# Hybrid decoder layer with expert retrieval: spare weight tiles first, fewer gathers beside the out-projection, one-hot rows on POOL, ids by a minimum

## Chip, cores and metric

The kernel runs on one core of one Trainium2 chip. The metric is the device time of one execution in microseconds (us), as a median over runs.

## What is computed

One decoder layer on 512 tokens of width 2048, in float32. Two token mixers of 16 heads each (latent attention with a rotary key, and forgetting attention) run side by side; their gated outputs are joined and projected, and an expert mixer with product keys follows.

```python
merged = jnp.concatenate([y_a, y_b], axis=-1) * gates          # (1, 512, 4096)
x = x + jnp.einsum('bse,ed->bsd', merged, w_out)               # 4096 -> 2048
h = rms_norm(x, ffn_norm_g)
q = (h @ w_q).reshape(T, 8, 2, 128)
scores = jnp.einsum('thcd,hcnd->thcn', q, sub_keys)            # 128 keys a half
s1, i1 = lax.top_k(scores[:, :, 0], 16)
s2, i2 = lax.top_k(scores[:, :, 1], 16)
top_scores, top_pos = lax.top_k(all 256 sums s1 + s2, 16)
experts = take_along_axis(i1 * 128 + i2, top_pos)              # of 16384 experts
gates = softmax(top_scores)
a = einsum('td,thkd->thk', h, u[experts])
x = x + einsum('thk,thkd->td', gates * gelu(a), v[experts])
```

## The kernel before, in words

Every matrix product is done with both operands split into a high and a low part, three matmuls each (mm3, L134). A weight tile of 128x1024 is loaded by SyncE (load, L97) into a slot "raw"; each half of 512 columns is cast by ACT to whi (L108), and DVE writes the rest to wlo (L113). There are three slots always, and spare (L607) opens two more for phase 2, with a split buffer of their own; loads go round over the five.

Phase 1 runs the attention heads; each head's gated output goes to DRAM (mrg, L319). Phase 2 (L561) is the out-projection. It handles the first block of 128 tokens apart: out0_units (L685) makes 128 units of three matmuls of 512 columns over all heads, the first 96 (early) of heads that are done first, the rest (late) after the last fourth of mrg was brought in. The other 384 tokens need 128 wide units ("main", out_units, L649), nine matmuls each; FEW of these stand among the late units. After the first block's norm come its queries, top-16 searches and expert choice (select, L802), with wide units between, and then the remaining main units. During them each half of a weight tile adds RATE to a credit (half_lo, L111), and each whole credit issues a gather: POOL fetches one expert row per token of the first block (1 MB), and DVE takes its dot product with the normalized input (L951) into aa. The credit begins at -LAG x RATE, and the last REST units issue no gather. All gathers that are left (352 in all) are spread over phase 4.

Phase 3 (L851) normalizes the other 384 tokens: DVE scales into hb (L869), PE transposes into tp, ACT and DVE split into dh and dl (L94, L95); then come queries and top-16 searches. select turns positions among 80 candidates into ids: for either key half a 128x6x16x16 tile is compared with the numbers 0 to 15 (L836), multiplied by the ids (L838) and summed over the last axis (L840).

Phase 4 begins with gate_matrix (L1006), whose order of instructions is that of the code. The ids and gates are transposed to "lists" (L1013, L1015). Then 84 groups of four tokens each: DVE compares the first id with 0 to 127 for three tokens (L1026), and for the fourth multiplies by the gate as well (L1028); it compares the second id for all four (L1030); ACT scales the first three (L1032); PE multiplies (L1045); ACT copies the result out (L1046); and once per four groups POOL copies eight rows to G (L1048) while the rest goes to DRAM. Between the groups LEFT "ahead" units (12 matmuls of 336 columns of the next product) are put in. Of 56 such units, FIRST = 32 run in phase 3, LEFT in the gate matrix, and the others after it. What follows is the product with all 16384 experts for 336 tokens, gated by that matrix.

Of the kernel before, what the change touches and what calls it, by code (L numbers as in the profile page):

```python
# [13 lines left out]
AF = mybir.ActivationFunctionType  # L14
OP = mybir.AluOpType
AX = mybir.AxisListType.X
# [3 lines left out]
P = 128  # L20
# [11 lines left out]
NKEY = 128  # L32
NEXP = NKEY * NKEY
TOPK = 16
# [17 lines left out]
ND = 3  # L52
# [10 lines left out]
NRAW2 = 2  # L63
NSP2 = 3
NC = 80
GATHERS = 2 * (128 + NX)
RATE = 0.46
REST = 10
LAG = 10
AHEAD = 14  # L70
# [3 lines left out]
FEW = 4  # L74
WAIT = 6
EACH = 8
FIRST = 32
LEFT = 4 * AHEAD - FIRST - 3
# [3 lines left out]
class Kern:  # L82
# [40 lines left out]
    def half(self, w, i):  # L123
        return self.half_lo(*self.half_hi(w, i))
# [436 lines left out]
    def phase2(self, res, sm):  # L561
        nc, a = self.nc, self.a
# [11 lines left out]
        with self.pool(name="mgr", bufs=1) as self.mgr, self.pool(name="msp", bufs=3) as self.msp, \  # L574
                self.pool(name="tka", bufs=1) as tk, self.spare(NRAW2, NSP2), \
# [3 lines left out]
            main = [f for q in range(4) for f in self.out_units(q, range(1, NT))]  # L579
# [105 lines left out]
    def out0_units(self, tk, main):  # L685
# [34 lines left out]
        out = early[:40] + [self.bare(own)] + early[40:64] + half(0) + early[64:] + [self.bare(bring, 3)]  # L720
        for i in range(0, len(late), 8):
            out += late[i:i + 8] + main[i // 8:i // 8 + 1] + (half(1) if i == 8 else [])
        return out
# [78 lines left out]
    def select(self, tk, vals, ids, n, gt, ie, eqs):  # L802
# [4 lines left out]
        nc.vector.tensor_copy(idf, ids)  # L807
        cand = tk.tile([P, n, NC // 8, 8], F32, name="cand")
# [25 lines left out]
        nc.vector.tensor_tensor(out=pf[:, 1], in0=slot, in1=w, op=OP.add)  # L834
        for c, eq in enumerate(eqs):
            nc.vector.tensor_tensor(out=eq, in0=pf[:, c, :, :, None].to_broadcast(bc),  # L836
                                    in1=iota[:, None, None, :].to_broadcast(bc), op=OP.is_equal)
            nc.vector.tensor_tensor(out=eq, in0=eq, in1=idf[:, c, :, None, :].to_broadcast(bc), op=OP.mult)  # L838
        for c, eq in enumerate(eqs):
            nc.vector.tensor_reduce(out=ie[:, c], in_=eq.rearrange("p (t h) a b -> p t h a b", t=nt), op=OP.add, axis=AX)  # L840
# [165 lines left out]
    def gate_matrix(self, pool, acc, ahead):  # L1006
        nc = self.nc
        lists = pool.tile([P, 3, TD], F32, name="lists")
        for b in range(ND):
            for j in range(3):  # L1010
                src = self.gt[:, b] if j == 2 else self.ie[:, j, b]
                tp = acc.tile([P, P], F32, name="acc")
                nc.tensor.transpose(tp, src.rearrange("p h k -> p (h k)"), self.ident)  # L1013
                o = NX if b == 0 else 0
                nc.scalar.copy(lists[:, j, b * P + o - NX:b * P + P - NX], tp[:, o:])  # L1015
        iota = self.cst[:, C_I2:C_I2 + P]
# [3 lines left out]
        b3 = [P, 3, NKEY]  # L1020

        def pick(g):
            t0 = 4 * g
            o1 = pool.tile(bc, F32, name="o1", bufs=3)
            o2 = pool.tile(bc, F32, name="o2", bufs=3)
            nc.vector.tensor_tensor(out=o1[:, :3], in0=lists[:, 0, t0:t0 + 3, None].to_broadcast(b3),  # L1026
                                    in1=iota[:, None, :].to_broadcast(b3), op=OP.is_equal)
            nc.vector.tensor_scalar(out=o1[:, 3], in0=iota, scalar1=lists[:, 0, t0 + 3:t0 + 4],  # L1028
                                    scalar2=lists[:, 2, t0 + 3:t0 + 4], op0=OP.is_equal, op1=OP.mult)
            nc.vector.tensor_tensor(out=o2, in0=lists[:, 1, t0:t0 + 4, None].to_broadcast(bc), in1=it, op=OP.is_equal)  # L1030
            for i in range(3):
                nc.scalar.activation(o1[:, i], o1[:, i], AF.Copy, scale=lists[:, 2, t0 + i:t0 + i + 1])  # L1032
            return o1, o2
# [252 lines left out]
```

## Time and profile before

| | |
|---|---|
| median of 3 runs | 4154.52 us (4152.19 to 4154.86) |
| the profiled execution | 4157.29 us, span 4155.5 us |
| mean granted clock | 0.989 |
| busy: PE, DVE, ACT, POOL | 4035.3, 3138.3, 1899.2, 642.0 us |
| attention, to about 1470 us | then the first out-projection to about 1612 us |
| main units with gathers | about 1700 to 1931 us |
| phase 3 | about 1931 to 2184 us |
| gate matrix | about 2184 to 2310 us |
| phase 4's products | to the end |

PE's busy time counts matmuls whose ends are modelled. An engine's idle time matters where PE waits for it; a gap of PE is read from the row that follows it, with the instruction that ended the wait. The rows are from one profiled execution, so sums are made against its own time.

### The profile page before, as it was taken

What the parts mean: (1) busy time and instruction counts of PE and PEld (TensorE: products, weight loads), DVE (VectorE), ACT (ScalarE), POOL (GpSimd) and SP (SyncE); (2) the same over time, 40 slices, a digit from 0 to 9 for tenths busy, and PEclk for the clock granted to TensorE, in tenths of its full rate; (3) what the DMA queues carried; (4) which work ended last, traced back from release to release, by engine and by line L of the source; (5) the groups of instructions that cost most, each with busy time, mean ns of one, the idle gap of its engine ahead of it and who ended that gap; (6) DMA issues with size and microseconds to landing.
All of it is one profiled execution on the core that took longest, in us unless ns stands there. A gap on an engine that the chain in (4) does not pass through costs nothing. (4 is left out here: it accounts for less than half of the span.)

```text
span 4155.5 us, 61144 instructions
## 1 busy us (share of the span) xinstructions
PE 4035.3 (97%) x22575; PEld 3633.3 (87%) x22575; DVE 3138.3 (76%) x5377; ACT 1899.2 (46%) x3677; POOL 642.0 (15%) x531
## 2 busy tenths in 40 slices
PE   8999999999999978998989999999999999999999
PEld 6878888888888756776989999999999999999998
DVE  8555655655555567888999888888888888888886
ACT  4555555555555555433339533333333333333332
POOL 1111101111111100022001112112221222122120
PEclk9999999999999989999999999999999999999999
DMA  3222222222222277698337898889889989899896
GB/s 134 88 77 82 79 82 82 86 74 85 81 86 79 84 265 261 245 357 319 116 118 201 313 341 334 338 340 348 336 332 347 339 334 347 343 327 356 323 340 211
DMA packets 246924, 937.94 MB, mean 226 GB/s; under 512 B 23760, under 2 KB 70864, under 8 KB 197840
## 3 DMA queue, kind: packets, MB, share of 16 engines
q1 hardware_dynamic: 190944, 550.11, 38.0%
q0 software_dynamic: 52160, 375.94, 23.9%
q10 hardware_dynamic: 3520, 7.98, 0.6%
q8 instruction: 177, 2.90, 0.3%
q14 instruction: 123, 1.01, 0.1%
HBM read 895.75 MB, written 38.14 MB: 225 GB/s over the span
## 5 line engine op out<-in xcount | busy, mean ns | idle before, releaser
L108 ACT CAST whi<-raw 128x512 fp32r<-128x512 f32 x1820 | 1111.1, 622 | 1745.7 <-PE acc L138 615.9
L113 DVE TENSOR_TENSOR wlo<-raw,whi 128x512 fp32r<-128x512 f32 x1820 | 1219.1, 687 | 523.4 <-ACT whi L108 510.9
L137 PE MATMUL acc<-Wh,whi 128*128 128x336 f32 x2048 | 642.2, 317 | 7.3 <-DVE x L1121 4.6
L138 PE MATMUL acc<-Wl,whi 128*128 128x336 f32 x2048 | 644.4, 316 | 0.0
L137 PE MATMUL a<-dh,whi 128*128 128x336 f32 x1984 | 629.2, 317 | 0.8 <-ACT whi L108 0.8
L138 PE MATMUL a<-dl,whi 128*128 128x336 f32 x1984 | 626.5, 316 | 0.0
L139 PE MATMUL a<-dh,wlo 128*128 128x336 f32 x1984 | 621.2, 316 | 0.9 <-DVE wlo L113 0.9
L139 PE MATMUL acc<-Wh,wlo 128*128 128x336 f32 x2048 | 607.7, 318 | 11.5 <-DVE wlo L113 11.0
L137 PE MATMUL mm<-hh,whi 128*128 128x512 f32 x1424 | 570.8, 401 | 8.3 <-ACT hh L540 8.3
L138 PE MATMUL mm<-hl,whi 128*128 128x512 f32 x1424 | 569.0, 400 | 6.5 <-DVE hl L541 6.4
L139 PE MATMUL mm<-hh,wlo 128*128 128x512 f32 x1424 | 569.1, 400 | 0.0
L137 PEld LDWEIGHTS acc<-Wh,whi 128*128 128x128 f32 x2048 | 384.8, 188 | 10.5 <-issue 6.6
L139 PEld LDWEIGHTS acc<-Wh,wlo 128*128 128x128 f32 x2048 | 375.7, 188 | 17.7 <-DVE wlo L113 17.5
L138 PEld LDWEIGHTS acc<-Wl,whi 128*128 128x128 f32 x2048 | 386.3, 189 | 0.0
L137 PEld LDWEIGHTS a<-dh,whi 128*128 128x128 f32 x1984 | 372.7, 188 | 2.2 <-ACT whi L108 1.4
L138 PEld LDWEIGHTS a<-dl,whi 128*128 128x128 f32 x1984 | 372.9, 188 | 0.0
L139 PEld LDWEIGHTS a<-dh,wlo 128*128 128x128 f32 x1984 | 371.3, 188 | 1.4 <-DVE wlo L113 1.4
L138 PEld LDWEIGHTS mm<-hl,whi 128*128 128x128 f32 x1424 | 268.6, 189 | 73.5 <-DVE hl L541 11.7
L137 PEld LDWEIGHTS mm<-hh,whi 128*128 128x128 f32 x1424 | 269.4, 189 | 67.8 <-ACT hh L540 8.3
L139 PEld LDWEIGHTS mm<-hh,wlo 128*128 128x128 f32 x1424 | 268.8, 189 | 60.9 <-issue 0.2
L951 DVE CUSTOM_DVE_ANT_0 rows<-rows,h 128x2048 f32<-128x2048 f32 x128 | 292.1, 2283 | 13.8 <-DMA rows<-u,eidx 13.8
L963 DVE SCALAR_TENSOR_TENSOR x<-rows,aa,x 128x2048 f32<-128x2048 f32 x128 | 300.1, 2345 | 0.0
(389 smaller groups left out, 6135.5 us busy)
## 6 DMA issues: line engine op xcount, KB each, us to landing
raw<-ut SPq DMA_DIRECT2D x256, 512.0 KB
raw<-vt SPq DMA_DIRECT2D x256, 512.0 KB
raw<-w_in SPq DMA_DIRECT2D x178, 512.0 KB
raw<-w_out SPq DMA_DIRECT2D x128, 512.0 KB
raw<-w_pq SPq DMA_DIRECT2D x64, 512.0 KB
gd<-rows SPq DMA_DIRECT2D x21, 1024.0 KB
G<-gd SPq DMA_DIRECT2D x15, 1344.0 KB
raw<-w_up SPq DMA_DIRECT2D x24, 512.0 KB
```

Source lines behind the costliest of these rows:

```text
L108: self.nc.scalar.copy(hi, src)
L113: ins = self.nc.vector.tensor_tensor(out=lo, in0=src, in1=hi.bitcast(F32), op=OP.subtract)
L137: nc.tensor.matmul(out, wh, xh, start=start, stop=False)
L138: nc.tensor.matmul(out, wh, xl, start=False, stop=False)
L139: nc.tensor.matmul(out, wl, xh, start=False, stop=stop)
L951: nc.vector.tensor_tensor_reduce(out=row, in0=row, in1=self.h0, scale=1.0, scalar=0.0, op0=OP.mult, op1=OP.add, accum_out=self.aa[:, k:k + 1])
L963: nc.vector.scalar_tensor_tensor(out=self.x1[0], in0=row, scalar=self.aa[:, k:k + 1], in1=self.x1[0], op0=OP.mult, op1=OP.add)
```

## The change

- The spare pool is opened before the other pools of phase 2, so that its tiles lie elsewhere in memory and the load order of the first tiles changes.
- Eight wide units (FEW) instead of four stand among the units of the first out-projection, one after every twelfth from the 36th on; the two halves of merged heads that they need are split at units 8 and 28.
- RATE is 0.40 instead of 0.46, and REST 14 instead of 10.
- select forms 256 times the position less (256 times the number plus the id), takes the absolute value on ACT and the minimum over the last axis, instead of a comparison, a multiplication and a sum.
- The lists are made in the order of kind and then of block, with an ahead unit after the second and the third kind. LEFT is 16 instead of 21.
- In the gate matrix POOL writes rows 2 and 3 of the first comparison together with the gate; DVE writes rows 0 and 1, which ACT scales.

```diff
@@ -64,18 +64,18 @@
 NSP2 = 3
 NC = 80
 GATHERS = 2 * (128 + NX)
-RATE = 0.46
-REST = 10
+RATE = 0.40
+REST = 14
 LAG = 10
 AHEAD = 14
 KEEP = 11
 LOOK = 1
 FIRST_W = {0: (0, 0), 2: (1, 0), 4: (0, 1), 6: (1, 1)}
-FEW = 4
+FEW = 8
 WAIT = 6
 EACH = 8
 FIRST = 32
-LEFT = 4 * AHEAD - FIRST - 3
+LEFT = 4 * AHEAD - FIRST - 8
 HALVES = 4 * NKEY + 4 * (NKEY - AHEAD) - 20
 
 
@@ -571,8 +571,8 @@
         self.gt = sm.tile([P, ND, PH, TOPK], F32, name="gt")
         self.ie = sm.tile([P, 2, ND, PH, TOPK], F32, name="ie")
         self.ss = sm.tile([P, NT, 4], F32, name="ss")
-        with self.pool(name="mgr", bufs=1) as self.mgr, self.pool(name="msp", bufs=3) as self.msp, \
-                self.pool(name="tka", bufs=1) as tk, self.spare(NRAW2, NSP2), \
+        with self.spare(NRAW2, NSP2), self.pool(name="mgr", bufs=1) as self.mgr, \
+                self.pool(name="msp", bufs=3) as self.msp, self.pool(name="tka", bufs=1) as tk, \
                 self.pool(name="pa", bufs=2, space=PSUM) as self.pa, \
                 self.pool(name="acc", bufs=6, space=PSUM) as self.accp:
             self.mhalf = {}
@@ -717,10 +717,18 @@
         for q in range(3):
             bring(q)
         half = lambda i: [self.bare(self.merged_half, 0, i)]
-        out = early[:40] + [self.bare(own)] + early[40:64] + half(0) + early[64:] + [self.bare(bring, 3)]
-        for i in range(0, len(late), 8):
-            out += late[i:i + 8] + main[i // 8:i // 8 + 1] + (half(1) if i == 8 else [])
-        return out
+        out, todo = [], main[:FEW]
+        for i, f in enumerate(early + late):
+            if i == len(early):
+                out.append(self.bare(bring, 3))
+            if i in (8, 28):
+                out += half(i // 20)
+            if i == 40:
+                out.append(self.bare(own))
+            out.append(f)
+            if i >= 36 and i % 12 == 0 and todo:
+                out.append(todo.pop(0))
+        return out + todo
 
     def inv_rms(self, pool, blocks, name):
         nc = self.nc
@@ -805,6 +813,9 @@
         nt = gt.shape[1]
         idf = tk.tile([P, 2, n, TOPK], F32, name="idf")
         nc.vector.tensor_copy(idf, ids)
+        nc.vector.scalar_tensor_tensor(out=idf.rearrange("p s n k -> p (s n) k"), scalar=2.0 * NKEY,
+                                       in0=iota[:, None, :].to_broadcast([P, 2 * n, TOPK]),
+                                       in1=idf.rearrange("p s n k -> p (s n) k"), op0=OP.mult, op1=OP.add)
         cand = tk.tile([P, n, NC // 8, 8], F32, name="cand")
         bc = [P, n, TOPK, TOPK]
         v1, v2 = vals[:, 0], vals[:, 1]
@@ -832,12 +843,13 @@
         nc.vector.tensor_tensor(out=w, in0=w, in1=lw, op=OP.subtract)
         nc.vector.tensor_scalar(out=slot, in0=slot, scalar1=1.0, scalar2=8.0, op0=OP.is_equal, op1=OP.mult)
         nc.vector.tensor_tensor(out=pf[:, 1], in0=slot, in1=w, op=OP.add)
+        nc.vector.tensor_scalar(out=pf, in0=pf, scalar1=2.0 * NKEY, scalar2=None, op0=OP.mult)
         for c, eq in enumerate(eqs):
             nc.vector.tensor_tensor(out=eq, in0=pf[:, c, :, :, None].to_broadcast(bc),
-                                    in1=iota[:, None, None, :].to_broadcast(bc), op=OP.is_equal)
-            nc.vector.tensor_tensor(out=eq, in0=eq, in1=idf[:, c, :, None, :].to_broadcast(bc), op=OP.mult)
+                                    in1=idf[:, c, :, None, :].to_broadcast(bc), op=OP.subtract)
+            nc.scalar.activation(eq, eq, AF.Abs)
         for c, eq in enumerate(eqs):
-            nc.vector.tensor_reduce(out=ie[:, c], in_=eq.rearrange("p (t h) a b -> p t h a b", t=nt), op=OP.add, axis=AX)
+            nc.vector.tensor_reduce(out=ie[:, c], in_=eq.rearrange("p (t h) a b -> p t h a b", t=nt), op=OP.min, axis=AX)
         b3 = [P, n, TOPK]
         g = tk.tile([P, n, TOPK], F32, name="g")
         nc.vector.tensor_tensor(out=g, in0=tv, in1=tv[:, :, 0:1].to_broadcast(b3), op=OP.subtract)
@@ -1006,29 +1018,32 @@
     def gate_matrix(self, pool, acc, ahead):
         nc = self.nc
         lists = pool.tile([P, 3, TD], F32, name="lists")
-        for b in range(ND):
-            for j in range(3):
+        for j in range(3):
+            for b in range(ND):
                 src = self.gt[:, b] if j == 2 else self.ie[:, j, b]
                 tp = acc.tile([P, P], F32, name="acc")
                 nc.tensor.transpose(tp, src.rearrange("p h k -> p (h k)"), self.ident)
                 o = NX if b == 0 else 0
                 nc.scalar.copy(lists[:, j, b * P + o - NX:b * P + P - NX], tp[:, o:])
+            if j:
+                next(ahead)
         iota = self.cst[:, C_I2:C_I2 + P]
         bc = [P, 4, NKEY]
         it = iota[:, None, :].to_broadcast(bc)
 
-        b3 = [P, 3, NKEY]
+        b2 = [P, 2, NKEY]
 
         def pick(g):
             t0 = 4 * g
             o1 = pool.tile(bc, F32, name="o1", bufs=3)
             o2 = pool.tile(bc, F32, name="o2", bufs=3)
-            nc.vector.tensor_tensor(out=o1[:, :3], in0=lists[:, 0, t0:t0 + 3, None].to_broadcast(b3),
-                                    in1=iota[:, None, :].to_broadcast(b3), op=OP.is_equal)
-            nc.vector.tensor_scalar(out=o1[:, 3], in0=iota, scalar1=lists[:, 0, t0 + 3:t0 + 4],
-                                    scalar2=lists[:, 2, t0 + 3:t0 + 4], op0=OP.is_equal, op1=OP.mult)
+            nc.vector.tensor_tensor(out=o1[:, :2], in0=lists[:, 0, t0:t0 + 2, None].to_broadcast(b2),
+                                    in1=iota[:, None, :].to_broadcast(b2), op=OP.is_equal)
+            for i in (2, 3):
+                nc.gpsimd.tensor_scalar(out=o1[:, i], in0=iota, scalar1=lists[:, 0, t0 + i:t0 + i + 1],
+                                        scalar2=lists[:, 2, t0 + i:t0 + i + 1], op0=OP.is_equal, op1=OP.mult)
             nc.vector.tensor_tensor(out=o2, in0=lists[:, 1, t0:t0 + 4, None].to_broadcast(bc), in1=it, op=OP.is_equal)
-            for i in range(3):
+            for i in range(2):
                 nc.scalar.activation(o1[:, i], o1[:, i], AF.Copy, scale=lists[:, 2, t0 + i:t0 + i + 1])
             return o1, o2
```

SyncE's queue at the start of the first out-projection, before (DMASW are loads and stores that POOL issued; the fifth row is the tile that the first unit needs):

```order
L101 DMA raw<-w_out 128x1024 [waits DMAHW7_50,DMASW0_50,DVE_50]
L101 DMA raw<-w_out 128x1024 [waits DMAHW0_50,DMASW1_50,DVE_50]
L101 DMA raw<-w_out 128x1024 [waits DMAHW1_50,DMAHW5_50,DMASW2_50,DVE_50]
L101 DMA raw<-w_out 128x1024 [waits DMAHW3_50,DVE_50]
L101 DMA raw<-w_out 128x1024 [waits DMASW5_50,DMASW4_50,DMAHW2_50,DVE_50,Pool_50]
L101 DMA raw<-w_out 128x1024 [waits Pool_50]
```

and with the change:

```order
L101 DMA raw<-w_out 128x1024 [waits Pool_50]
L101 DMA raw<-w_out 128x1024 [waits PE_50]
L101 DMA raw<-w_out 128x1024 [waits DMAHW5_50,DMAHW7_50,DMASW0_50,DVE_50]
L101 DMA raw<-w_out 128x1024 [waits DMAHW0_50,DMASW1_50,DVE_50]
L101 DMA raw<-w_out 128x1024 [waits DMAHW1_50,DMASW2_50,DVE_50]
L101 DMA raw<-w_out 128x1024 [waits DMAHW3_50,DVE_50]
```

The two tiles of the spare slots moved from fifth and sixth to first and second, and wait for POOL and for PE instead of for POOL's stores and loads.

DVE around the norm of phase 3, before (ISA rows,aa is one dot of a gathered row; n1r the norm; hb, dl and dh as in phase 3):

```order
L951 ISA rows,aa<-rows,h_14565 128x2048
L951 ISA aa 128x1
L729 TENSOR_REDUCE n1r<-ss 128x3
L148 SCALAR_TENSOR_TENSOR rsq<-n1r,rsq 128x3
L150 TENSOR_TENSOR n1y<-n1y,rsq 128x3
L869 SCALAR_TENSOR_TENSOR hb<-x_13376,n1y,hb 128x512 x3
L951 ISA rows,aa<-rows,h_14565 128x2048
L951 ISA aa 128x1
L951 ISA rows,aa<-rows,h_14565 128x2048
L951 ISA aa 128x1
L95 TENSOR_TENSOR dl<-tp,dh 128x384 x3
L113 TENSOR_TENSOR wlo<-raw,whi 128x512
```

and with the change:

```order
L963 ISA rows,aa<-rows,h_14626 128x2048
L963 ISA aa 128x1
L678 TENSOR_TENSOR x_13376<-x_13376,acc 128x512 x3
L737 TENSOR_REDUCE n1r<-ss 128x3
L148 SCALAR_TENSOR_TENSOR rsq<-n1r,rsq 128x3
L150 TENSOR_TENSOR n1y<-n1y,rsq 128x3
L881 SCALAR_TENSOR_TENSOR hb<-x_13376,n1y,hb 128x512 x3
L95 TENSOR_TENSOR dl<-tp,dh 128x384 x3
L113 TENSOR_TENSOR wlo<-raw,whi 128x512
L95 TENSOR_TENSOR dl<-tp,dh 128x384
L881 SCALAR_TENSOR_TENSOR hb<-x_13376,n1y,hb 128x512 x3
L113 TENSOR_TENSOR wlo<-raw,whi 128x512 x3
```

All dots now stand ahead of the norm; in the rows before, nine stood behind it, the last ones between later pieces of hb and dl.

DVE in the gate matrix, before (o is either one-hot tile, by its number):

```order
L1026 TENSOR_TENSOR o_19962<-lists,cst 128x384
L1028 TENSOR_SCALAR o_19962<-cst,lists 128x128
L1030 TENSOR_TENSOR o_19963<-lists,cst 128x512
L1026 TENSOR_TENSOR o_19970<-lists,cst 128x384
L1028 TENSOR_SCALAR o_19970<-cst,lists 128x128
L1030 TENSOR_TENSOR o_19971<-lists,cst 128x512
```

and with the change, DVE first:

```order
L1040 TENSOR_TENSOR o_19989<-lists,cst 128x256
L1045 TENSOR_TENSOR o_19990<-lists,cst 128x512
L1040 TENSOR_TENSOR o_19997<-lists,cst 128x256
L1045 TENSOR_TENSOR o_19998<-lists,cst 128x512
L1040 TENSOR_TENSOR o_20006<-lists,cst 128x256
L1045 TENSOR_TENSOR o_20007<-lists,cst 128x512
```

and POOL, where the rows before held only one COPY per four groups:

```order
L1043 TENSOR_SCALAR o_20350<-cst,lists 128x128 x2
L1043 TENSOR_SCALAR o_20380<-cst,lists 128x128 x2
L1043 TENSOR_SCALAR o_20394<-cst,lists 128x128 x2
L1043 TENSOR_SCALAR o_20408<-cst,lists 128x128 x2
L1063 COPY G<-rows 128x128
```

One DVE instruction per group is gone and one is shorter, and two POOL instructions per group were added.

## Rows read from the trace of the kernel before

**Rows 1.** The page: busy time, share of the span and instructions of each engine.
```profile
PE 4035.3 (97%) x22575; PEld 3633.3 (87%) x22575; DVE 3138.3 (76%) x5377; ACT 1899.2 (46%) x3677; POOL 642.0 (15%) x531
```

**Rows 2.** Stretches: length, busy PE, PEld, DVE, ACT, POOL, granted clock, DMA share, GB/s.
```profile
1440.00:1460.00 20.00, 14.43 (x74) 11.35 (x72) 13.19 (x28) 10.38 (x24) 2.47 (x3) 0.91 0.51 171
1460.00:1480.00 20.00, 8.14 (x22) 4.81 (x21) 5.33 (x9) 3.60 (x8) 1.70 (x3) 0.50 0.40 132
1480.00:1500.00 20.00, 16.65 (x58) 11.95 (x59) 12.33 (x19) 10.99 (x19) 0.00 (x0) 0.82 0.68 223
1500.00:1540.00 40.00, 37.23 (x150) 26.52 (x150) 32.52 (x51) 29.31 (x51) 0.00 (x0) 1.00 0.91 324
1540.00:1620.00 80.00, 70.23 (x277) 51.64 (x275) 57.76 (x99) 49.24 (x92) 0.91 (x1) 0.96 0.84 295
```

**Rows 3.** Waits of SyncE's queue, 1430 to 1490, and PE's timeline row there.
```profile
SPq L101 <- DMA mrg<-gate: 15.9, 1, 15.9
...
1482.49 0.80 PE L137 MATMUL pa<-whi,m 128*128 128x512 f32 x1 [10.45 <-ACT whi L108]
```

**Rows 4.** Stretches, waits of PE, and DVE's timeline, all from 1920 to 2000.
```profile
1920.00:1960.00 40.00, 26.62 (x119) 22.02 (x117) 30.28 (x41) 11.01 (x26) 7.03 (x8) 0.79 0.91 354
1960.00:2000.00 40.00, 34.34 (x201) 32.86 (x200) 33.23 (x60) 14.65 (x28) 3.64 (x4) 0.96 0.57 195
...
PE tp L875 <- DVE dl L95: 11.6, 3, 6.9
PE tp L875 <- DVE hb L869: 5.4, 1, 5.4
...
1939.29 2.29 DVE L951 CUSTOM_DVE_ANT_0 rows<-rows,h 128x2048 f32<-128x2048 f32 x1 [1.41 <-DMA rows<-u,eidx]
...
1944.75 2.29 DVE L951 CUSTOM_DVE_ANT_0 rows<-rows,h 128x2048 f32<-128x2048 f32 x1 [3.16 <-DMA rows<-u,eidx]
```

**Rows 5.** Stretch, DVE timeline, PE wait and ACT's queue at the selects.
```profile
2000.00:2160.00 160.00, 154.35 (x936) 152.29 (x935) 159.97 (x715) 59.72 (x109) 0.00 (x0) 0.99 0.37 116
...
2167.87 1.75 DVE L838 TENSOR_TENSOR hb<-hb,idf 128x1536 f32<-128x1536 f32 x1
...
PE acc L1013 <- ACT lists L1015: 5.1, 1, 5.1
...
2176.36 5.64 ACTq L919 DMA_DIRECT2D idxx<-idx  x9
```

**Rows 6.** Gate matrix: the stretch, groups of DVE instructions, POOL's timeline.
```profile
2200.00:2300.00 100.00, 98.86 (x739) 95.50 (x737) 99.62 (x218) 100.00 (x288) 13.35 (x17) 1.00 0.76 217
...
L1030 DVE TENSOR_TENSOR o<-lists,cst 128x512 f32<-128x512 f32 x83 | 56.2, 677 | 0.0
...
L1026 DVE TENSOR_TENSOR o<-lists,cst 128x384 f32<-128x384 f32 x82 | 45.1, 550 | 0.6 <-issue 0.4 <-ACT o L1032 0.2
...
2215.23 1.32 POOL L1048 COPY G<-rows 128x128 f32<-128x128 f32 x1 [5.92 <-ACT rows L1046]
...
2221.18 1.28 POOL L1048 COPY G<-rows 128x128 f32<-128x128 f32 x1 [4.63 <-ACT rows L1046]
```

**Rows 7.** DVE and POOL together: timelines, the source view of L1048, a POOL group.
```profile
566.24 1.76 DVE L457 TENSOR_TENSOR raw<-raw,rbc 128x512 f32<-128x512 f32 x1
...
566.17 1.29 POOL L460 TENSOR_TENSOR raw<-kg,rbc 64x512 f32<-64x512 f32 x1 [0.19 <-POOL rbc L150]
...
2215.85 0.54 DVE L1026 TENSOR_TENSOR o<-lists,cst 128x384 f32<-128x384 f32 x1
...
L1048 POOL COPY G<-rows x21: 295/595/1322, 2191.1 to 2309.4; 128x128 f32<-128x128 f32 x21
...
L263 POOL TENSOR_SCALAR raw<-raw 128x512 f32<-128x512 f32 x32 | 54.2, 1692 | 430.8 <-ACT raw L262 430.2
```

**Rows 8.** Stretch of phase 4, and the group of dots from 1600 to 2000.
```profile
2340.00:4100.00 1760.00, 1744.75 (x11266) 1733.50 (x11265) 1489.62 (x1868) 661.95 (x1176) 374.90 (x317) 1.00 0.90 337
...
L951 DVE CUSTOM_DVE_ANT_0 rows<-rows,h 128x2048 f32<-128x2048 f32 x41 | 93.5, 2281 | 4.6 <-DMA rows<-u,eidx 4.6
```

## Prediction

> **What bounds the kernel now.** The page's totals come first: TensorE (PE) is busy for 4035.3 of 4155.5 us [rows 1], so every gain has to come out of about 120 us in which it idles, and of stretches at a lower granted clock. The table of stretches says where these lie. From 1440 to 1620 us, from the last attention head through the first out-projection, PE is busy for 14.43 + 8.14 + 16.65 + 37.23 + 70.23 = 146.7 of 180 us [rows 2], so 33.3 us are idle; the granted clock of 0.91, 0.50, 0.82 and 0.96 in four of these rows costs a further 14.43 x 0.09 + 8.14 x 0.50 + 16.65 x 0.18 + 70.23 x 0.04 = 11.2 us. That makes 44.5 us, the ceiling for this stage. From 1920 to 2000 the same sum gives 19.0 us idle and 7.0 us of clock [rows 4]. The gate matrix is of another kind: from 2200 to 2300 VectorE (DVE) and ScalarE (ACT) are both busy for practically 100 of 100 us [rows 6], so there the helpers set the pace. In phase 4 PE is busy for 1744.75 of 1760 us [rows 8], with the DMA share already at 0.90.
>
> The waits then name the causes. In the first stage the longest single one is 10.45 us before the first pa matmul, which waits for the cast of the first w_out tile; SyncE's queue had held that load for 15.9 us until the gate output of the last head was stored [rows 3]. At 1920 PE waits 11.6 us for dl and 5.4 us for hb [rows 4], where DVE runs dots of gathered rows (L951, 2.28 us each) between the pieces of the normalized input, and idles for the gather itself before two of them (1.41 and 3.16 us).
>
> **The first out-projection.** With the spare pool placed first, its two tiles no longer lie on what the last head stores; the order shows their loads as SyncE's first two, waiting for POOL and PE work of earlier heads alone. The 10.45 us wait then goes. What follows is late next: the loads. 1460 to 1620 moved 20 x 132 + 20 x 223 + 40 x 324 + 80 x 295 = 43.7 MB [rows 2]. At 324 GB/s, the rate of the row that is fullest (share 0.91), this takes 135 us and ends at 1595, 25 us earlier. Two more w_out tiles (the four additional wide units) cost 1.05 MB, 3 us; the two tiles that now arrive before 1460 give as much back. The four wide units are 36 matmuls of work taken from later: at 37.23 / 150 = 0.248 us each [rows 2], 9 us that PE need not do afterwards. Sum: **34 us gained**. Bounds: 10 (the single wait) and 44.5 (the ceiling). I take 34, since the share of 0.91 says that the loads, and not PE, set the end of this stage.
>
> **Fewer gathers beside the main units.** 0.46 x 100 units less the lag gave 41 dots before 2000 [rows 8]; 0.40 x 92 less the lag gives 32, and the order shows all of these ahead of the norm. Between the first hb and the first dl this removes 1.41 + 2.29 + 3.16 + 2.29 = 9.2 us [rows 4], and one dot of 2.3 us ahead of the norm. Some 3 us of the 7 us lost to the clock, which fell after PE had idled there, should return: **14 us gained**, between 5 (the transposes still wait for their splits) and 20 (nearly all of 26). The nine dots go to phase 4: 9 x 2.28 = 21 us of DVE, which is busy for 1489.6 of 1760 us there, and 9 x 1.05 MB, 28 us at 337 GB/s, where a tenth of the DMA time is free [rows 8]. The cover is that free tenth, 176 us; I charge **2 us**, with 0 and 28 as bounds.
>
> **Ids by a minimum.** Each select loses two multiplications of 1.75 us on DVE [rows 5] and gets two short DVE instructions on 192 columns and two Abs of 1536 columns on ACT. No row shows such an Abs; a DVE pass over the same shape takes 1.75 us, and zero is the other end. From 2000 to 2160 DVE is busy throughout, but PE too for 154 of 160 us, so only the chain of the last select is exposed: 3.5 us less, and one Abs more that the second subtraction does not cover. **3 us gained**, between a loss of 2 and a gain of 8. ACT's issue of nine copies of idxx, 5.64 us, still stands ahead of most list copies, and PE's wait of 5.1 us at the lists [rows 5] is filled by two ahead units.
>
> **The gate matrix.** Today 84 groups take 125 us: POOL's copies, one per four groups, start at 2215.23 and 2221.18 [rows 6], so 5.95 x 21. Per group DVE loses its L1028 instruction and a third of L1026, ACT loses one of three scalings, and POOL gets two tensor_scalar of 128x128. If POOL were free, the bound would be PE: 84 x 8 matmuls of L1045 and 16 units of 12 are 864, and at 98.86 / 739 = 0.134 us each [rows 6] that is 116 us, somewhat too much, since the ends of matmuls are modelled.
>
> But POOL is not free. DVE's L457, two operands from SBUF, lasts 1.76 us instead of about 0.68 while POOL's L460 runs, and ends 0.54 us after it; POOL's copy, 0.295 us at best, takes 1.32 us at 2215.23 and ends 0.16 us after DVE's L1026 does [rows 6, 7]. So the second of the two is held for as long as the first runs, and only its start, about 0.13 us, is hidden. I therefore add up both engines. A group holds DVE for 0.545 (512 columns), 0.29 (256 columns: 0.423 us on the line between L1026 and L1030, less 0.13) and 0.10 (the unit's wlo, 16/84 of 0.545): 0.94 us. POOL's new instruction has no row. The copy of the same shape holds for 0.295 - 0.13 = 0.165 us; L263, the same kind of instruction on 512 columns with a mean of 1.692 us [rows 7], gives a quarter of 1.56, 0.39. One shares the shape, the other the kind, and neither is nearer; I take the middle, 0.28. Then 0.94 + 2 x 0.28 + 0.04 = 1.54 us a group, 129 us, **4 us lost**; the ends give 110 and 148 us. Five units leave the stage, two for the lists, three for after it. At 12 x 1744.75 / 11266 us [rows 8] the three take 5.6 us, of which I charge half, the rest filling idle time: **3 us lost**.
>
> The Trainium skill (SBUF — State Buffer, Who interferes with whom) calls this an exclusive lock: a DVE instruction with two SBUF inputs contends with a GpSimd instruction that reads SBUF, and the one that comes second is blocked outright. The trace agrees (1.32 us for a copy of 0.295). By that rule, with nothing of either instruction hidden, the sum is that of the first rival; by the held times of the rows it is 129 us.
>
> **Sum.** -34 - 14 + 2 - 3 + 4 + 3 = -42 us. The profiled execution took 4157.3 us, 2.8 above the median of the three runs, so 4115.3 there and 4112.5 as a median.
>
> **Rivals.**
> *POOL and DVE take turns with whole instructions (slower).* Then a group is 0.68 + 0.42 + 0.13 on DVE, 2 x 0.52 on POOL (0.39 and a start of 0.13) and 0.07 for the copy: 2.34 us, 197 us, a loss of 72 + 3. Everything else gains 49, so the end is 26 us later: 4180. It decides from 2.04 us a group. For it: POOL waits of 1.3 us today. Against it: DVE's L1026 beside the copy at 2215.85 took 0.54 us, its usual time [rows 7].
> *POOL is cheap.* At the copy's price POOL and DVE need 110 us and PE up to 116, so 113: 12 us gained instead of 4 lost, 58 in all, 4096. For it: the same shape today, 0.295 us at best.
> *The loads bind sooner.* If the early tiles only take the 10.45 us wait away, because DMA fills up earlier and the later stretch (295 GB/s) does not speed up, the first stage gives 10.5 instead of 34: 4136. For it: the share is 0.84 to 0.91 after 1500 already.
> *The moved gathers cost their full time in phase 4.* 28 instead of 2 us: 4138. Against it: PE idles less than 1% there.
>
> **How the numbers follow.** Forecast 0.42, cheap POOL 0.20, loads 0.18, gathers 0.08, whole instructions 0.12. The range reaches from 4082 (cheap POOL and the ceiling of the first stage) to 4162 (the last three bounds together, short of the slower rival). About 0.2%, 8.3 us, is what a measurement of this kernel can tell from no change. Faster takes the first four cases but for the part where two of them meet, 0.79; same 0.09; slower 0.12.
>
> **What would show it.** Right: the first pa matmul before 1475 us, beside the last head; w_out arriving at 320 GB/s without a gap from 1460 to about 1595; no L951 row between hb and dl; gate-matrix copies 5.2 to 6.5 us apart, with POOL instructions that last well over 0.4 us when they meet DVE. Wrong: copies 8 us or more apart; w_out loads still waiting for stores; PE idle over 2% in phase 4.

## The result, and the profile after

The changed kernel took 4202.76 us (median of 4 runs, 4199.01 to 4204.22), the kernel before 4153.75 us on the same chip: a ratio of 1.0117, with a 95% interval of 1.0102 to 1.0133. It is 49 us slower. The forecast was 41 us faster, and the time lies outside the range. The profiled execution has a span of 4197.2 us, 41.7 more than before. Sums over stretches below are made between profiled executions.

The page of the changed kernel, busy time by engine; it answers to [rows 1].

```profile
PE 4065.3 (97%) x22575; PEld 3655.3 (87%) x22575; DVE 3100.8 (74%) x5293; ACT 1893.5 (45%) x3603; POOL 825.0 (20%) x699
```

POOL has 183 us more (825.0 against 642.0 us). The stretches of the same execution, with the columns of [rows 2]:

```profile
1440.00:1460.00 20.00, 16.05 (x79) 12.79 (x78) 12.86 (x28) 10.45 (x25) 3.21 (x3) 0.88 0.59 211
1460.00:1480.00 20.00, 19.15 (x88) 15.25 (x87) 17.90 (x32) 15.49 (x31) 0.64 (x1) 0.95 0.89 320
1480.00:1500.00 20.00, 16.55 (x67) 11.83 (x65) 16.04 (x26) 14.08 (x25) 1.08 (x2) 1.00 0.99 383
1500.00:1540.00 40.00, 35.61 (x141) 25.53 (x141) 26.57 (x43) 23.03 (x42) 0.00 (x0) 1.00 0.82 274
1540.00:1620.00 80.00, 71.35 (x290) 51.99 (x289) 56.50 (x96) 45.91 (x87) 0.91 (x1) 0.98 0.77 256
```

```profile
1920.00:1960.00 40.00, 38.62 (x228) 37.41 (x227) 23.29 (x38) 15.85 (x30) 0.00 (x0) 0.97 0.43 137
1960.00:2000.00 40.00, 39.85 (x242) 39.26 (x241) 38.57 (x184) 18.26 (x33) 0.00 (x0) 1.00 0.34 106
2000.00:2160.00 160.00, 151.91 (x937) 148.21 (x935) 141.67 (x591) 77.25 (x146) 21.16 (x19) 0.98 0.39 119
2160.00:2200.00 40.00, 30.64 (x177) 28.41 (x178) 19.73 (x38) 21.81 (x56) 39.02 (x41) 0.82 0.49 137
2200.00:2300.00 100.00, 77.22 (x436) 71.87 (x436) 49.21 (x94) 54.39 (x138) 97.71 (x97) 0.79 0.45 130
```

The gap at 1460 to 1480 is closed (19.15 us of PE instead of 8.14), and the dip of 1920 to 2000 as well (78.5 of 80 us instead of 61.0 [rows 4]). But from 2160 to 2300 PE is busy for 107.9 of 140 us at a granted clock of about 0.8, DVE and ACT are half idle, and POOL is busy throughout: 97.71 of 100 us in the last row, where before it had 13.35 [rows 6].

Landmarks show where the time went. In each of the two blocks below, of the kernel before and of the changed one, the first two rows are the norms of the first block and of the others, and the third is the gate matrix on PE (the source view: least, median and greatest duration in ns, then first and last start).

```profile
L729 DVE TENSOR_REDUCE n0r<-ss x1: 156/156/156, 1611.9 to 1611.9; 128x1 f32<-128x4 f32 x1
L729 DVE TENSOR_REDUCE n1r<-ss x1: 159/159/159, 1934.1 to 1934.1; 128x3 f32<-128x12 f32 x1
...
L1045 PE MATMUL acc<-o,o x672: 270/275/579, 2184.1 to 2308.4; 128*128 128x128 f32 x168
```

```profile
L737 DVE TENSOR_REDUCE n0r<-ss x1: 157/157/157, 1601.9 to 1601.9; 128x1 f32<-128x4 f32 x1
L737 DVE TENSOR_REDUCE n1r<-ss x1: 166/166/166, 1913.8 to 1913.8; 128x3 f32<-128x12 f32 x1
...
L1060 PE MATMUL acc<-o,o x672: 270/275/582, 2140.4 to 2335.1; 128*128 128x128 f32 x168
```

| stretch, us | before | changed | difference |
|---|---|---|---|
| to the norm of the first block | 1611.9 | 1601.9 | -10.0 |
| to the norm of the others | 322.2 | 311.9 | -10.3 |
| to the gate matrix | 250.0 | 226.6 | -23.4 |
| gate matrix | 124.3 | 194.7 | +70.4 |
| to the end of the span | 1847.1 | 1862.1 | +15.0 |

So 43.7 us were gained ahead of the gate matrix, where 51 were forecast; the gate matrix took 70 us back, and phase 4 a further 15. Landmarks of single executions differ by some us without any cause in the code: in the three kernels below that are the kernel before up to there (POOL's rows alone, the rate, the minimum) the first norm stands at 1608.6 to 1609.5, not at 1611.9, and with POOL's rows alone the gate matrix starts at 2179.4, not at 2184.1. Some 5 of the 43.7 us may be such spread.

What POOL did in the gate matrix is seen in two views, the group with its mean, and the source view with minimum, median and maximum; the last row is DVE's longer instruction.

```profile
L1043 POOL TENSOR_SCALAR o<-cst,lists 128x128 f32<-128x128 f32 x168 | 184.6, 1111 | 238.8 <-DMA raw<-ut 236.6 <-PE acc L1060 1.3 <-issue 0.8
...
L1043 POOL TENSOR_SCALAR o<-cst,lists x168: 782/793/2007, 2138.8 to 2333.8; 128x128 f32<-128x128 f32 x168
...
L1045 DVE TENSOR_TENSOR o<-lists,cst x84: 676/683/860, 2138.5 to 2328.5; 128x512 f32<-128x512 f32 x84
```

The 52 of the 168 that met no DVE instruction took 0.782 to 0.797 us; called 0.785 us alone in what follows. The 100 that met DVE's one-hot rows took 1.154 us on the mean, the 16 that met a wlo as well 1.88, and the longest 2.0; that makes 1.11 us over all. DVE's instruction hardly feels it (0.683 us as a median, 0.676 at best). PE's waits from 2130 to 2340 have one cause, but for 0.5 us:

```profile
PE acc L1060 <- POOL o L1043: 44.9, 48, 1.9
```

### The profile page after: what moved, and what is told of

It reads as the page before. It is cut to its first block, busy times and chain, and to the rows that moved or that the text cites. A ratio compares the mean times of both kernels' runs of the same rounds, so it can differ in the third digit from the quotient of the medians.

```text
span 4197.2 us, 61251 instructions
## 1 busy us (share of the span) xinstructions
PE 4065.3 (97%) x22575; PEld 3655.3 (87%) x22575; DVE 3100.8 (74%) x5293; ACT 1893.5 (45%) x3603; POOL 825.0 (20%) x699
## 5 line engine op out<-in xcount | busy, mean ns | idle before, releaser
L137 PE MATMUL a<-dh,whi 128*128 128x336 f32 x1984 | 637.8, 322 | 1.1 <-ACT whi L108 1.1
L139 PE MATMUL a<-dh,wlo 128*128 128x336 f32 x1984 | 630.3, 320 | 4.9 <-DVE wlo L113 4.6
L139 PE MATMUL acc<-Wh,wlo 128*128 128x336 f32 x2048 | 603.4, 318 | 15.2 <-DVE wlo L113 14.7
```

Of the source, the lines that this page charges most:

```text
L137: nc.tensor.matmul(out, wh, xh, start=start, stop=False)
L139: nc.tensor.matmul(out, wl, xh, start=False, stop=stop)
```

## The experiments

Two theories stood against each other from the start. *POOL:* the two instructions a group, with DVE in turn, cost the time, and the rest of the change gains. *The rest:* the early loads, the gathers or the new lists lose as well, and POOL is only part of it.

**The rows written as before.**

```diff
-            nc.vector.tensor_tensor(out=o1[:, :2], ...)
-            for i in (2, 3):
-                nc.gpsimd.tensor_scalar(out=o1[:, i], ...)
+            nc.vector.tensor_tensor(out=o1[:, :3], ...)
+            nc.vector.tensor_scalar(out=o1[:, 3], ...)
...
-            for i in range(2):
+            for i in range(3):
                 nc.scalar.activation(o1[:, i], ...)
```

> The changed kernel with one thing undone: the one-hot rows are written as before (DVE three rows and the fourth with its gate, ACT scales three), POOL only copies G. Theory (POOL's two instructions a group and the turns they take with DVE cost the time): the gate matrix goes from 198 us back to about 122 to 125, so the whole to 4130 +- 8 us. Rival (the other parts lose as well, the early gathers or the loads): over 4150 us.

Measured: 4141.16 us, the kernel before 4152.64 on that chip, a ratio of 0.9973 (0.9961 to 0.9986). The gate matrix took 121.3 us, 73 fewer than in the changed kernel, as the theory had it. The whole fell between the two expectations, since phase 4 became longer still:

```profile
L1059 PE MATMUL acc<-o,o x672: 270/275/377, 2143.1 to 2264.4; 128*128 128x128 f32 x168
...
core 0: 4137.8 us, clock 0.992
```

From the last start of the gate matrix to the end it takes 1873.4 us, where it was 1847.1 before. That needed runs of its own (below).

**POOL's rows alone, in the kernel before.**

```diff
-            nc.vector.tensor_tensor(out=o1[:, :3], ...)
-            nc.vector.tensor_scalar(out=o1[:, 3], ...)
+            nc.vector.tensor_tensor(out=o1[:, :2], ...)
+            for i in (2, 3):
+                nc.gpsimd.tensor_scalar(out=o1[:, i], ...)
```

> The kernel before with this one thing added: POOL writes two of the four one-hot rows. Theory: 84 groups of 2.3 us instead of 1.49, so 68 to 73 us longer, 4222 to 4227 us. Rival (the gate matrix suffers from the new order of the lists and the ahead units, not from POOL): under 4175 us.

```profile
L1029 POOL TENSOR_SCALAR o<-cst,lists x168: 780/788/2050, 2177.8 to 2374.9; 128x128 f32<-128x128 f32 x168
...
L1046 PE MATMUL acc<-o,o x672: 270/275/583, 2179.4 to 2376.2; 128*128 128x128 f32 x168
```

Measured: 4223.21 us, a ratio of 1.0171 (1.0154 to 1.0188), or 70.6 us more, as expected. The gate matrix runs from 2179.4 to 2376.2 us, 196.8. The rival falls: POOL's rows account for the loss by themselves, with the lists and the ahead units as they were.

**What makes the instruction dear? Plain numbers in place of its operands.** This kernel leaves the ids and gates out of two of four rows, so it does not compute the layer.

```diff
-                nc.gpsimd.tensor_scalar(out=o1[:, i], in0=iota, scalar1=lists[:, 0, ...],
-                                        scalar2=lists[:, 2, ...], op0=OP.is_equal, op1=OP.mult)
+                nc.gpsimd.tensor_scalar(out=o1[:, i], in0=iota, scalar1=5.0,
+                                        scalar2=0.5, op0=OP.is_equal, op1=OP.mult)
```

> The changed kernel, but POOL's two instructions compare with 5 and multiply by 0.5 instead of the id and the gate of each partition, so two of four one-hot rows hold wrong values. If the operands that are read per partition make them dear (0.785 us alone, where a quarter of L263's 1.69 us would be 0.42), they fall to about 0.5 us, a group to 1.7 us, the whole to about 4150 us. If it is the instruction with two operations itself, they stay near 0.78 us and the whole near 4203 us.

```profile
L1043 POOL TENSOR_SCALAR o<-cst x168: 640/642/1104, 2127.7 to 2290.4; 128x128 f32<-128x128 f32 x168
...
L1060 PE MATMUL acc<-o,o x672: 270/275/579, 2142.9 to 2291.4; 128*128 128x128 f32 x168
```

Measured: 4157.12 us, 46 below the changed kernel (1.0010 of the kernel before, 1.0000 to 1.0019). Neither expectation holds in full. The two operands per partition make 0.145 of the 0.785 us, and the instruction with two operations still takes 0.64, not 0.5. What makes the 0.64 was not run: no kernel here has the instruction at this shape with one operation. A group takes 148.5 / 84 = 1.77 us, where the prediction's sum of held times gives 0.94 + 2 x (0.64 - 0.13) + 0.04 = 2.00, so that sum does not hold here. The mean of POOL's instruction is 0.758 us in the stage, so each waits 0.12 us and not 0.33 as in the changed kernel; why so much less was not followed.

**DVE with one operand from SBUF.**

```diff
-            nc.vector.tensor_tensor(out=o1[:, :2], in0=lists[:, 0, ...], in1=iota..., op=OP.is_equal)
+            for i in (0, 1):
+                nc.vector.tensor_scalar(out=o1[:, i], in0=iota, scalar1=lists[:, 0, ...], ..., op0=OP.is_equal)
...
-            nc.vector.tensor_tensor(out=o2, in0=lists[:, 1, ...], in1=it, op=OP.is_equal)
+            for i in range(4):
+                nc.vector.tensor_scalar(out=o2[:, i], in0=iota, scalar1=lists[:, 1, ...], ..., op0=OP.is_equal)
```

> The changed kernel, but DVE writes its rows by six tensor_scalar of 128 columns (the ids as a number per partition) instead of two tensor_tensor with two operands from SBUF; POOL's two instructions stay. Theory (DVE's second operand and POOL exclude each other): POOL's instruction falls from a mean of 1.11 us to about 0.79, a group to about 1.65 us, set by POOL (2 x 0.79) or DVE (6 x 0.26), and the whole to 4143 +- 8 us, although DVE has more to do. Rival (POOL's instruction is slow in this stage for another reason): its mean stays over 1.0 us and the whole at 4195 us or more.

```profile
L1044 POOL TENSOR_SCALAR o<-cst,lists 128x128 f32<-128x128 f32 x168 | 153.3, 923 | 237.3 <-DVE o L1047 237.3
...
L1044 POOL TENSOR_SCALAR o<-cst,lists x168: 780/894/1436, 2139.4 to 2297.8; 128x128 f32<-128x128 f32 x168
...
L1063 PE MATMUL acc<-o,o x672: 270/275/582, 2140.9 to 2299.2; 128*128 128x128 f32 x168
```

Measured: 4169.42 us, 33 below the changed kernel, between the two expectations. DVE has six instructions a group instead of two, and yet the gate matrix is shorter, 158.3 us: POOL's mean falls from 1.11 to 0.92 us. So the form of DVE's instructions made much of POOL's wait. It does not fall to 0.79, and the trace shows both sources of what is left: the 18 of POOL's instructions that met no DVE instruction took 0.785 us on the mean, the 130 that met only one-operand rows 0.891, and the 20 that met a wlo, which still has two operands, 1.257. Beside the rows alone that is 0.891 instead of 1.154 us. The edit also made each of DVE's instructions shorter (0.29 to 0.30 us as a median instead of 0.43 and 0.68), so the number of operands and the length were changed together, and which of them counts is not shown.

**The other parts, each alone in the kernel before.** First the spare pool with the new order and eight wide units (the diff of the change), then the pool alone, whose diff is this; the blocks below come in the same order.

```diff
-        with self.pool(name="mgr", bufs=1) as self.mgr, ..., self.spare(NRAW2, NSP2), \
+        with self.spare(NRAW2, NSP2), self.pool(name="mgr", bufs=1) as self.mgr, ...
```

> The kernel before with the spare pool first, and eight wide units in the new order of the first out-projection; nothing else. Theory: the first block's norm comes 10 us earlier with four more wide units done (9 us), so 4135 +- 5 us. Rival (the loads take it back later, in the queries or in phase 3): 4148 us or more.

> The kernel before with the spare pool first, the order of units and the four wide units as before. If the early loads bring the gain, 4138 +- 5 us; if it needs the wide units between the loads (the loads pace the stage, so PE has no more to do in it), 4143 to 4150 us.

```profile
L737 DVE TENSOR_REDUCE n0r<-ss x1: 136/136/136, 1600.3 to 1600.3; 128x1 f32<-128x4 f32 x1
L737 DVE TENSOR_REDUCE n1r<-ss x1: 161/161/161, 1909.4 to 1909.4; 128x3 f32<-128x12 f32 x1
```

```profile
L729 DVE TENSOR_REDUCE n0r<-ss x1: 136/136/136, 1588.7 to 1588.7; 128x1 f32<-128x4 f32 x1
L729 DVE TENSOR_REDUCE n1r<-ss x1: 161/161/161, 1913.3 to 1913.3; 128x3 f32<-128x12 f32 x1
```

Measured: 4132.12 us with both and 4138.77 with the pool alone, where the kernel before had 4156.15; ratios of 0.9951 (0.9934 to 0.9967) and 0.9962 (0.9948 to 0.9976). Both are as expected. The pool alone, and with it the early loads, brings 17 of the 24 us; the two intervals overlap, so a gain from the wide units is not shown. With four wide units the first block's norm comes at 1588.7, 23 us earlier than before; with eight it comes at 1600.3, as PE does 36 matmuls more by then (9 us). The profiled execution with eight (4120.50 us) is the fastest of its four, 12 us below the median.

**Rate and rest.**

```diff
-RATE = 0.46
-REST = 10
+RATE = 0.40
+REST = 14
```

> The kernel before with RATE 0.40 and REST 14 only. Theory: 13 us gained around the norm of phase 3, 8 us given back in phase 4 where nine more gathers run, so 4149 +- 4 us. Rival (the moved gathers are free, as forecast): 4140 us. Second rival (they cost their full 28 us of DMA time): 4168 us.

PE's waits for wlo in phase 4, before and here:

```profile
PE acc L139 <- DVE wlo L113: 11.0, 13, 1.8
```

```profile
PE acc L139 <- DVE wlo L113: 17.9, 22, 2.9
```

Measured: 4153.43 us, a ratio of 0.9996 (0.9986 to 1.0006): no change that shows. The gate matrix starts at 2178.7, 5.4 us earlier, but the kernel with POOL's rows alone, the same as before up to there, starts it at 2179.4, so this gain is not shown. Phase 4 takes 1852.8 us instead of 1847.1, and there PE waits 17.9 us for wlo instead of 11.0.

**Ids by a minimum.** The diff is that of select in the change.

> The kernel before with the ids by a minimum only (list order and units as before). Forecast: 3 us gained, 4151 us. Rival (DVE's 12 us less in the selects count in full, since DVE was busy throughout there): 4142 us. Second rival (ACT's Abs holds up the casts): 4156 us.

```profile
L729 DVE TENSOR_REDUCE n1r<-ss x1: 159/159/159, 1932.0 to 1932.0; 128x3 f32<-128x12 f32 x1
...
L1049 PE MATMUL acc<-o,o x672: 270/276/378, 2163.5 to 2287.8; 128*128 128x128 f32 x168
...
L842 ACT ACTIVATE hb<-hb 128x1536 f32<-128x1536 f32 x8 | 11.9, 1488 | 0.5 <-DVE hb L840 0.3
```

The first top-16 search of phase 3 (the first start of the MAX8 row) and the last sum or minimum of select (the last start of the other) bound the selects, before and here:

```profile
L795 DVE MAX8 vals<-sc x48: 264/274/296, 1997.2 to 2137.5; 128x8 f32<-128x128 f32 x48
L840 DVE TENSOR_REDUCE ie<-hb x10: 1732/1744/2276, 1745.4 to 2170.7; 128x96 f32<-128x1536 f32 x8, 128x128 f32<-128x2048 f32 x2
```

```profile
L795 DVE MAX8 vals<-sc x48: 271/277/297, 1987.8 to 2119.5; 128x8 f32<-128x128 f32 x48
L844 DVE TENSOR_REDUCE ie<-hb x10: 1730/1749/2279, 1745.4 to 2149.0; 128x96 f32<-128x1536 f32 x8, 128x128 f32<-128x2048 f32 x2
```

Measured: 4138.59 us, a ratio of 0.9958 (0.9941 to 0.9974), 17.6 us less, against 3 forecast. From the norm to the gate matrix it takes 231.5 us instead of 250.0, 18.5 less. The selects have 12.3 of these (161.2 us instead of 173.5). DVE lost eight multiplications of 1.75 us there, 14.0, and got eight short instructions, 2.4 in all, so it has 11.6 us less to do: the first rival of this run held, and DVE's saving counted in full. Another 7.3 us went between the norm and the first search (55.8 us instead of 63.1), where the code is as before; PE waits 3.7 us for dl there instead of 11.6, and why was not followed. Abs takes ACT 1.49 us, and no row shows that PE waits for it.

**Can the gains be kept, and what of phase 4?** Four kernels, all with the spare pool first, eight wide units, ids by a minimum, and the rows as before. Against the first experiment above they differ in these lines:

```diff
-RATE = 0.40
-REST = 14
+RATE = 0.46
+REST = 10
...
-LEFT = 4 * AHEAD - FIRST - 8
+LEFT = 4 * AHEAD - FIRST - 5
```

In order: the first of the four has both edits, with LEFT at 21 and the lists made in the old order, without ahead units among them; the second has both edits; the third has that of LEFT alone (19); the fourth that of the rate alone.

> The kernel before with the spare pool first, eight wide units and the ids by a minimum; gathers, list order, ahead units and gate matrix as before. If the two parts add up (24 and 17 us apart), about 4114 us; if they meet in the same stretch (phase 3, where fewer wide units and a shorter DVE both help), 4120 to 4132 us.

> As the last one, with the new order of the lists and two ahead units in it, three after the gate matrix as before (LEFT 19). The gate matrix has two units fewer and ACT 1 us less, PE's wait of 5 us at the lists is filled: 2 to 4 us less than without. Rival: the same time, since the lists still end behind ACT's issues.

> The changed kernel with the rows written as before and LEFT 19 instead of 16, so three ahead units after the gate matrix instead of six. If the three units that were moved behind the gate matrix cost there (5.6 us of PE, and they were hidden inside), 4135 us against 4141 with 16; if not, 4141.

> The changed kernel with the rows written as before and RATE 0.46, REST 10 as before. If the nine gathers that moved to phase 4 cost it most of the 26 us by which phase 4 is longer than before when the rows are written as before (1869 against 1843 us), phase 4 falls to 1850 us or less and the whole to 4125 to 4132 us. If they were free, 4141 us or more, since the norm of phase 3 waits again.

The first row of the table is the first experiment, with rate and LEFT of the change; the four follow.

| kernel (rate, LEFT) | median, us | ratio to before (95%) | gate matrix to end, us |
|---|---|---|---|
| 0.40, 16 | 4141.16 | 0.9973 (0.9961 to 0.9986) | 1873.4 |
| 0.46, 21, old lists | 4123.57 | 0.9923 (0.9905 to 0.9941) | 1850.1 |
| 0.46, 19 | 4123.06 | 0.9925 (0.9908 to 0.9941) | 1851.4 |
| 0.40, 19 | 4126.17 | 0.9933 (0.9917 to 0.9950) | 1857.8 |
| 0.46, 16 | 4119.01 | 0.9912 (0.9895 to 0.9929) | 1840.6 |

The parts did not add up: the first two of them, 24 and 17.6 us apart, give 30.3 together, for both shorten the way from the norm to the gate matrix: from 250.0 to 239.2 and 231.5 us apart, and no further than 229.8 together. The lists made no difference that shows, as the rival of that run had it. LEFT 19 instead of 16 gained 15 us at rate 0.40, where 6 were expected at most, and the fourth kernel came out below its range. With rate 0.46 the whole is 22 us faster at LEFT 16 and 3 us at LEFT 19. PE's waits in phase 4 and the stretch itself (columns of [rows 2]), for rate 0.40 and then 0.46, both with LEFT 16:

```profile
PE acc L139 <- DVE wlo L113: 15.2, 19, 1.8
PE acc L137 <- ACT whi L108: 7.4, 5, 4.0
PE acc L1014 <- DVE h L1006: 4.6, 1, 4.6
...
2265.00:4137.00 1872.00, 1834.64 (x11763) 1812.77 (x11761) 1561.88 (x1972) 683.78 (x1222) 411.22 (x332) 0.99 0.89 333
```

```profile
PE acc L139 <- DVE wlo L113: 4.9, 4, 1.7
PE acc L137 <- ACT whi L108: 3.5, 2, 2.5
...
2279.00:4118.00 1839.00, 1819.84 (x11761) 1808.41 (x11759) 1545.50 (x1958) 681.63 (x1222) 369.33 (x325) 1.00 0.90 335
```

At rate 0.40 PE waits for wlo 19 times instead of 4, and 15.2 us instead of 4.9, and DVE has more dots and additions of gathered rows between (39 gathers ahead of the gate matrix with 0.46 here, 32 with 0.40). A single wait of 4.6 us for the last extra rows at the end comes on top. But waits are only part of the 33 us between these two: 14.8 us are busy time of PE, longer for practically the same matmuls, at a mean granted clock of 0.99 instead of 1.00. And the wait for wlo does not set the stretch by itself, as with rate 0.40 and LEFT 19 it is longer still, in a stretch that is 15.6 us shorter:

```profile
PE acc L139 <- DVE wlo L113: 18.1, 22, 1.8
```

What makes up the rest, and why the three units behind the gate matrix cost with one rate and not with the other, stays open. The kernel with 0.46 and 16 beats both kernels of this study, by 35 and 84 us.

## Why the prediction was wrong, point by point

- **The gate matrix: forecast 4 us lost in the stage itself, measured 70.** The step that failed is the price of POOL's instruction: "I take the middle, 0.28". It was to lie between the copy's 0.165 and the 0.39 of a quarter of L263 [rows 7]; alone it takes 0.785, so it holds for 0.655 us, more than the upper bound. A quarter of a long instruction was no bound for a short one with two operations and operands that differ by partition: taking the operands away only brought it to 0.64. With 0.655 the forecast's own sum gives 0.94 + 1.31 + 0.04 = 2.29 us a group, 192 us; measured were 194.7. In the kernel with POOL's rows alone it gives 2.32 and 2.34 were measured, but with plain numbers 2.00 against 1.77. So the price was off by 2 x 0.375 x 84 = 63 us, which is nearly all of the miss in this stage; that the held times of both engines add up fits here and is no rule. The sign of being wrong came too: the copies stand (2336.2 - 2152.0) / 20 = 9.2 us apart, where 8 was named.
- **Who waits.** I wrote that "the second of the two is held". In this stage the wait fell on POOL nearly alone, 1.11 us as a mean against 0.785, with DVE at its usual times: 79 of the 84 shorter instructions (L1040) began while one of POOL's ran, and took 0.426 us as a median, no more than the four that began ahead of POOL's. And the engine that POOL starved was PE (44.9 us). The trace of before had it already: POOL's copy at 2215.23 [rows 6] began ahead of this instruction of DVE and of the one at 2215.85 [rows 7], and ended behind both, so that it was held and DVE, which came second, was not.

```profile
2215.25 0.67 DVE L1030 TENSOR_TENSOR o<-lists,cst 128x512 f32<-128x512 f32 x1
```

  Even without any wait POOL would have needed 168 x 0.785 + 7.8 = 140 us, more than the 125 of before.
- **The first rival gave 197 us and 2.34 us a group**, practically what was measured, from a higher price (0.52 for the whole instruction, still below the measured 0.785) and whole instructions instead of held times. That it came out right was luck: with 0.785 its own sum is 0.68 + 0.42 + 0.13 + 1.57 + 0.07 = 2.87 us a group. Its condition, over 2.04 us a group, was met.
- **The first out-projection: forecast 34, measured about 20** (10.0 at the first norm with 9 us of additional work done, 20.3 at the second), and 24 with nothing else changed (14 to 27 by the interval). The wait of 10.45 us went, as forecast. The step that failed is "324 GB/s, the rate of the row that is fullest". The rate was reached between 1460 and 1500 (320 and 383 GB/s), while slots were free, and not held after it (274 and 256). SyncE's queue was by then waiting for slots:

```profile
SPq L101 <- DVE wlo L113: 69.3, 46, 4.3
```

  Of 100 us it waited 69.3 for a slot that the split had to free; before it was 65.9 of the same 100. That fits a stage paced by the round of five slots, load, cast, split and the next load, with neither DMA nor PE full (shares of 0.77 to 0.82, and 0.89); no run varied the slots, so it is argued and not shown.
- **Fewer gathers: forecast 14 gained and 2 given back.** Alone the step changed nothing that shows in the time, and the cover that was charged with 2 us is the step that failed: phase 4 took 5.7 us more, and a free tenth of its DMA time did not help, as it is for DVE's wlo that PE waits there (17.9 us instead of 11.0). Nor did the gain come. In that run PE still waited 12.3 us for hb and dl, instead of 17.0, as 34 gathers were issued and the last dots still stood around the norm; in the whole change, with four wide units fewer left for gathers, 4.9 us of wait remain.
- **Ids by a minimum: forecast 3, measured 17.6 alone.** "PE too for 154 of 160 us, so only the chain of the last select is exposed" was the wrong step. PE's busy time counts matmuls with modelled ends; DVE, busy for 159.97 of 160 us [rows 5], was the bound. Phase 3 lost eight multiplications there, 11.6 us of DVE with the short instructions that came in, and the selects became 12.3 us shorter. The other 7.3 us, ahead of the selects, no part of the forecast or of a rival foresaw.
- Ahead of the gate matrix errors of opposite sign nearly cancelled (51 forecast, 43.7 measured), so that the sum was nearly right with wrong parts. The first pa matmul stood at 1458 us, as forecast, beside the last head.
- **Phase 4: forecast 5 lost with the three units, measured 15.** Over that stretch PE is busy for 1827.99 us instead of 1818.52, 9.5 more, with the 36 matmuls of the three units in it, and idle for 5.5 more; its wait for wlo grew from 11.0 to 14.7 us. What made the busy time grow by more than the 5.6 us of the three units is open.
- **The range.** Its lower end does not come out of its terms: 4096, less the 10.5 us between the ceiling of 44.5 and the 34, is 4086 and not 4082. Its upper end, 4162, holds two of the rivals (23.5 and 26 us more), not three.

The Trainium skill (SBUF — State Buffer, Who interferes with whom) has it that a DVE instruction with at most one SBUF input, outside the two-port modes, does not contend with GpSimd. The run with one operand agrees in direction, POOL's mean 0.92 against 1.11 us, but not in full: beside one-operand rows alone it is 0.891, and with no DVE instruction beside it 0.785. Whether those rows ran outside the two-port modes, so that the rule covers them, no run here shows. The section's other rule, which the prediction drew on, that the one that comes second is blocked, does not describe these rows: POOL was held though it had begun first.

## What to carry to other kernels

Before work is moved to an engine that is idle, measure the one new instruction there in its exact form; the engine's low share says nothing of its price, and bounds from other shapes and operations can both lie below it. Where POOL and DVE work side by side, look for the one that has to wait, here POOL; adding up their held times was a good estimate in two runs and 0.23 us a group too high in a third. An engine that is busy for 159.97 of 160 us was the bound even where PE seemed 96% busy beside it, and the 11.6 us taken off it made the stretch 12.3 us shorter.

## What the hardware showed that was not expected

- A POOL tensor_scalar of 128x128 float32 with two operations took 0.785 us with operands per partition and 0.640 with plain numbers, a copy of the same shape 0.287 (the median of L1063), and DVE's instruction of the same kind 0.333 us (L1028 in the kernel before).

```profile
L1063 POOL COPY G<-rows x21: 281/287/732, 2152.0 to 2336.2; 128x128 f32<-128x128 f32 x21
...
L1028 DVE TENSOR_SCALAR o<-cst,lists 128x128 f32<-128x128 f32 x83 | 27.6, 333 | 0.0
```

- When POOL and DVE met in the gate matrix, POOL's instructions grew from 0.785 to as much as 2.0 us, and DVE's hardly did (0.683 against 0.676).
- PE's granted clock was 0.79 from 2200 to 2300, a mean between its levels of 1.2 and 2.4 GHz, while PE waited for POOL and was busy for 77.22 of 100 us; in the same stage before it was 1.00, the upper level, with 98.86 of 100 us busy.
